# A two-block transformer on one core: adaLN units of four strips in a row, heads of a pair in alternation

## The chip, the core and the metric

The kernel runs on one core of one Trainium2 chip. A core has a matrix engine (PE, whose weight loads are listed apart as PEld), a vector engine (DVE), an activation engine (ACT), a general engine (POOL) and an engine that here only starts transfers (SP); each has its own instruction stream and they meet through semaphores. The metric is the device time of one execution in microseconds (us), the median of several runs of the same program.

## The reference, cut to what matters

Two blocks run one after the other on 256 positions of width 1024. The first has two layers, each with adaLN vectors, a mixer (convolution and a chunked state-space scan, "ssd") and a mixture of experts; its first layer also runs the same on 256 context positions. The second block has four layers, of which the first and the last are forgetting attention ("fox").

```python
def ada_mod(cvec, w_ada, b_ada, n):            # 1024 -> 6 vectors of 1024
    m = jax.nn.silu(cvec) @ w_ada[:, :n * D_MODEL] + b_ada[:n * D_MODEL]
    return jnp.split(m, n, axis=-1)

def first_block(...):
    for l in range(2):
        sh1, sc1, gt1, sh2, sc2, gt2 = ada_mod(c, w_ada[l], b_ada[l], 6)
        # the context: the same with c_ctx
        hx = modulate(rms_norm(h_x, g_mix[l]), sh1, sc1)
        u, gate, z, xbc, dt_raw = split_proj(hx @ p["w_in"])
        xs, bm, cm, dt = ssd_scan_inputs(xbc, dt_raw, p)
        h_x = h_x + gt1 * mixer_output(u, gate, z, xs, bm, cm, dt, a, hf0, hb0, p, rows)
        h_x = h_x + gt2 * hier_moe(modulate(rms_norm(h_x, g_ffn[l]), sh2, sc2), p)
        ...

def ssd_chunked(...):                          # within mixer_output, 8 heads of 64, both directions
    scores = jnp.einsum("bclhn,bcshn->bclsh", cc, bc) * decay_ls
    y_diag = jnp.einsum("bclsh,bcshp->bclhp", scores, xdt)
    ...

def forgetting_attention(h, w_in, b_f, w_out): # 16 heads of 64
    logits = jnp.einsum('bhqd,bhkd->bhqk', q_b, k) * scale
    logits = logits + c_b[..., :, None] - c[..., None, :]
    p = jax.nn.softmax(jnp.where(mask, logits, -jnp.inf), axis=-1)
    return jnp.einsum('bhqk,bhkd->bhqd', p, v) @ w_out
```

## The kernel before

**Arithmetic.** Large products are made of three matmuls of split operands (`mm3`, L45 on): high by high, high by low, low by high. The high part `wh` of a weight is written by ACT from the loaded tile `raw` (L54), the low part `wl` mostly by DVE (L55). All matmuls go through `mm` (L45, L46), so that rows of the profile on them carry L46 and are told apart by the tile they write. A plain fp32 matmul leaves two records on PE, one such as `proj<-xh,wh` one.

**adaLN units.** `ada(l)` (L199) computes silu(c) times `w_ada`: the stationary operand is `sc32`, 128 by 32 (two vectors and 30 zero columns), the moving one a strip of `w_ada`, 128 by 512. A bank of PSUM (`adaps`) takes four strips, one in each quarter of its partitions, that is in each quarter of the array's columns. The generator yields after two strips: this is a *unit* of the kernel before, and two units use one 1 MB load of `w_ada`. `fill(n)` (L264) takes n units and so puts them between other matmuls, wherever it is called: in `load_x`, twice in each projection of the first layer (`proj`, `k in (2, 6)`), in the first layer's ssd, its router and its experts, then in the second layer's z projections, ssd and router. With `hold` (and always at the last of a block) the partial sums leave PSUM for `adar`, by a copy on ACT (L252) or an addition on DVE (L250); `turn` then transposes them into the vectors `AD`.

**ssd.** `head` is a generator of three steps, one for each of 8 heads and stream: step 1 starts the decay logits `L` (a matmul from `pick`), step 2 adds the mask and has ACT write six exponentials into `es` (four slots, L706) which DVE multiplies with `pg`; step 3 multiplies them with `xdt` into `py`. Two heads (a *pair*) share one bank `py`: head e writes partitions 64e to 64e+63, by four matmuls of 64 stationary columns. Three heads are in flight; each step 3 stands by itself in the stream.

**fox.** `heads` handles a pair: for each head in turn `pick`, `cmask` and two `qk` matmuls (64 rows contracted, head e in rows 64e to 64e+63) into a bank of its own; softmax; three transposes per head; and the product with v into one bank, head e in partitions 64e on. Four banks are enough, so the pair's three parts are interleaved with those of the next pair by the caller.

**Order.** A scheduler places instructions in program order with priorities and waits; PE's order, the place of every unit among it, is thus set by where `fill` is called. `moe0` also pins one `fill(1)` behind an instruction (`issue_after(self.placed.ins)`). The experts' weights, the adaLN weights and all others are loaded by one queue of SP in program order into a ring of `raw` buffers.

Of the kernel before, what the change touches and what calls it, by code (L numbers as in the profile page):

```python
# [16 lines left out]
P = 128  # L17
# [12 lines left out]
class Net:  # L30
# [131 lines left out]
    def load_x(self):  # L162
# [8 lines left out]
        self.fill(3)  # L171
# [3 lines left out]
        for k in range(KC):  # L175
            self.ssq_add(k)
            self.fill(1)
# [5 lines left out]
        self.fill(5)  # L183
# [15 lines left out]
    def ada(self, l):  # L199
# [9 lines left out]
        def turn(b, a0, a1):  # L209
# [6 lines left out]
            for a in range(a0, a1):  # L216
                nc.vector.tensor_tensor(o[:, a], pt[:, a, :, 0:2], pv["b_ada"][:, 16 * b + 4 * a:16 * b + 4 * a + 4, None].to_broadcast([P, 4, 2]), op=ALU.add)
            if b != 1 and a0 == 0:
# [4 lines left out]

        blocks = [(b, range(4)) for b in range(3)] if l == 0 else [(0, range(4)), (1, range(4)), (2, range(2)), (2, range(2, 4))]
        for b, groups in blocks:
            groups, n = list(groups), len(groups)
            ps, taken = None, set()

            for k in range(KC):
                for h in range(n // 2):  # L230
                    self.ada_flush()
                    if ps is None:
                        ps, begun = self.pm.tile([P, 512], F32, name="adaps", tag=self.mmtag), set()
                    if h == 0 and (n == 4 or k % 2 == 0):
                        c0 = 2048 * b + 512 * groups[0]
                        r = self.raw(w[:, k:k + 4 // n, c0:c0 + 512 * n], 4 // n, 512 * n)
                    rr = r[:, 0 if n == 4 else k % 2].rearrange("p (g n) -> p g n", n=512)
                    for g in (2 * h, 2 * h + 1):
                        a = groups[g]
                        self.mm(ps[32 * a:32 * a + 32], self.sc32[:, k], rr[:, g], a not in begun, k == KC - 1)  # L240
                        begun.add(a)
                    done = k == KC - 1 and h == n // 2 - 1
                    if done or self.hold:
                        for old in (False, True):
                            part = [a for a in begun if (a in taken) == old]
                            if part:
                                at = slice(32 * min(part), 32 * max(part) + 32)
                                o = rows[at].rearrange("p j n -> p (j n)")
                                if old:
                                    nc.vector.tensor_tensor(o, o, ps[at], op=ALU.add)  # L250
                                else:
                                    nc.scalar.activation(o, ps[at], AF.Copy)  # L252
                        taken |= begun
                        ps = None
                    if done:
                        self.turns.append((turn, b, groups[0], groups[-1] + 1))
                    yield
# [60 lines left out]
    def mixer(self, l):  # L318
# [36 lines left out]
        l0 = [True] + 35 * [False]  # L355
# [33 lines left out]
        for a in range(4):  # L389
            r = self.raw(win[:, :, 1536 + 256 * a:1792 + 256 * a], KC, 256)  # L390
            for b in range(2):
# [5 lines left out]
                if last:  # L397
                    self.fill([0, 0, 0, 0, 0, 0, 0, 0][c])
        for a in range(2):
            r = self.raw(win[:, :, 1024 + 256 * a:1280 + 256 * a], KC, 256)  # L400
            for b in range(2):
# [5 lines left out]
                if last:  # L407
                    self.fill([1, 1, 1, 1][2 * a + b])
# [22 lines left out]
        if last:  # L431
            self.fill(88 - self.units, True)
# [185 lines left out]
    def ssd(self, l, xbc, xdt, cz, dt, dta, rows, NS, ssq, conv, cnorm):  # L618
# [75 lines left out]
        pgs, pys, later = {}, {}, []  # L694

        def head(n, s, c, e):
# [21 lines left out]
            if e == 0:  # L718
                pys[s, c] = pm.tile([P, T], F32, name="py", tag="mm")
            py = pys[s, c]  # L720
            o = py[64 * e:64 * e + 64]
# [1578 lines left out]
```

## Time and profile before

| what | value |
|---|---|
| median of 3 runs | 2184.17 us (2183.2 to 2184.49) |
| the profiled execution | 2185.32 us, its span 2183.5 us |
| PE busy | 2021.5 us, 93% of the span |
| DVE / ACT / POOL busy | 68% / 47% / 20% |
| adaLN matmul records | 384, 89.0 us busy |

The span is the stretch from the first to the last instruction of the profiled execution. PE's busy share is over 99% in long stretches and lower in the first layer's ssd, around the routers and in the second layer's experts. An engine's end of a matmul is modelled, so for what a group of matmuls costs the start of the next instruction on PE is read, not the group's own duration.

### The profile page before, as it was taken

The numbers are of one execution on the slowest core, as the hardware profiler recorded it, in microseconds if no ns is written. First come the engines' busy times: TensorE is split into PE (matmuls) and PEld (weight loads), VectorE is DVE, ScalarE is ACT, GpSimd is POOL, SyncE is SP. The second block draws the span as 40 slices with busy tenths as digits, with TensorE's granted clock in tenths as the row PEclk, the third lists the DMA queues.
The fourth block names the chain that finished last, engine by engine and source line by source line (L and its number), as shares of the span: only waits on it lengthen the run. The fifth ranks groups of instructions, "written<-read, shape, count | busy, mean of one in ns | idle before, by whom it ended". The sixth has DMA issues, their size and how long they took to land.

```text
span 2183.5 us, 37025 instructions
## 1 busy us (share of the span) xinstructions
PE 2021.5 (93%) x14917; PEld 1713.7 (78%) x14919; DVE 1475.4 (68%) x2429; ACT 1034.8 (47%) x1743; POOL 434.4 (20%) x574
## 2 busy tenths in 40 slices
PE   6999896999898989789989997799999999999998
PEld 3655563998586656368889996699998999989998
DVE  4878646999798541069766669976658556667664
ACT  4323543887543631056554452254456444546444
POOL 1000212232433210022268832200001000010000
PEclk9999997999999999999999999799999999999999
DMA  7553414999434479964456653255544554425551
GB/s 297 212 193 117 155 58 150 323 343 338 139 121 149 157 267 366 375 224 155 155 174 203 200 181 103 89 193 174 183 165 136 192 193 157 136 97 195 195 190 39
DMA packets 276595, 408.89 MB, mean 187 GB/s; under 512 B 9856, under 2 KB 241280, under 8 KB 270144
## 3 DMA queue, kind: packets, MB, share of 16 engines
q1 hardware_dynamic: 266976, 380.47, 51.5%
q0 software_dynamic: 8000, 19.67, 2.5%
q10 hardware_dynamic: 1440, 6.29, 0.7%
q8 instruction: 120, 1.97, 0.4%
q14 instruction: 59, 0.48, 0.1%
HBM read 390.93 MB, written 24.64 MB: 190 GB/s over the span
## 4 chain that ended last, share of the span: by engine, by line
PE 48%; DVE 8%; DMA 2%; issue 2%; ACT 2%; POOL 1%; SPq 0%; DVEq 0%; POOLq 0%; ACTq 0%
PE mm L46 43%; DVE wl L55 2%; PE gu L46 2%; PE py L46 1%; DVE Z L2146 1%; DMA raw<-in_w_down 1%; DMA rawe<-in_w_down 1%; PE px L46 1%; DVE gl L1552 1%; DVE A L2139 0%; PE mm L1778 0%; DVE A L2148 0%; PE acc L46 0%; POOL Z L2141 0%; DMA bc<-bcd 0%
## 5 line engine op out<-in xcount | busy, mean ns | idle before, releaser
L54 ACT ACTIVATE wh<-raw 128x1024 fp32r<-128x1024 f32 x490 | 511.1, 1050 | 494.1 <-PE mm L46 274.5
L55 DVE TENSOR_TENSOR wl<-raw,wh 128x1024 fp32r<-128x1024 f32 (+2 forms) x478 | 586.5, 1232 | 223.8 <-ACT wh L54 222.5
L46 PE MATMUL mm<-gh,wh 128*128 128x256 f32 (+1 forms) x1744 | 496.9, 285 | 2.4 <-ACT wh L54 2.4
L46 PE MATMUL mm<-gh,wl 128*128 128x256 f32 (+1 forms) x1744 | 494.0, 283 | 2.3 <-DVE wl L55 2.3
L46 PE MATMUL mm<-gl,wh 128*128 128x256 f32 (+1 forms) x1744 | 493.7, 283 | 0.5 <-DVE gl L1552 0.5
L46 PEld LDWEIGHTS mm<-gh,wh 128*128 128x128 f32 (+1 forms) x1744 | 329.8, 189 | 5.4 <-ACT wh L54 2.6
L46 PEld LDWEIGHTS mm<-gh,wl 128*128 128x128 f32 (+1 forms) x1744 | 329.3, 189 | 3.7 <-DVE wl L55 2.9
L46 PEld LDWEIGHTS mm<-gl,wh 128*128 128x128 f32 (+1 forms) x1744 | 329.6, 189 | 2.2 <-DVE gl L1552 0.9
L46 PE MATMUL mm<-fh,wh 128*128 128x256 f32 x704 | 199.0, 286 | 3.0 <-DVE x L1592 1.6
L46 PE MATMUL mm<-fl,wh 128*128 128x256 f32 x704 | 198.7, 283 | 0.0
L46 PE MATMUL mm<-fh,wl 128*128 128x256 f32 x704 | 198.2, 283 | 0.0
L1556 POOL TENSOR_TENSOR sq<-sq 128x256 f32<-128x256 f32 x48 | 41.2, 859 | 682.7 <-ACT sq L1554 482.5
L46 PEld LDWEIGHTS mm<-fh,wh 128*128 128x128 f32 x704 | 134.2, 192 | 5.1 <-DVE x L1592 2.4
L46 PEld LDWEIGHTS mm<-fl,wh 128*128 128x128 f32 x704 | 134.9, 192 | 0.1
L46 PEld LDWEIGHTS mm<-fh,wl 128*128 128x128 f32 x704 | 134.6, 192 | 0.0
L46 PE MATMUL proj<-xh,wl 128*128 128x512 f32 (+1 forms) x320 | 116.5, 365 | 11.0 <-POOL xr L534 7.7
L46 PE MATMUL proj<-xh,wh 128*128 128x512 f32 (+1 forms) x320 | 120.5, 377 | 1.7 <-ACT wh L54 1.7
L46 PE MATMUL proj<-xl,wh 128*128 128x512 f32 (+1 forms) x320 | 115.4, 361 | 0.0
L46 PE MATMUL gu<-wh,gt 128*128 128x256 f32 x512 | 98.3, 286 | 0.2 <-DVE gt L55 0.2
L46 PE MATMUL adaps<-raw,sc 128*32 128x512 f32 x384 | 89.0, 627 | 9.9 <-DVE sc L170 7.2
L1618 DVE TENSOR_TENSOR ft<-mm,rstd 128x512 f32<-128x512 f32 x88 | 60.8, 691 | 53.3 <-PE mm L46 53.3
L46 PEld LDWEIGHTS proj<-xh,wh 128*128 128x128 f32 x320 | 62.3, 195 | 43.1 <-issue 30.1
(596 smaller groups left out, 4130.7 us busy)
## 6 DMA issues: line engine op xcount, KB each, us to landing
raw<-in_ffn_w_gate_up SPq DMA_DIRECT2D x88, 1024.0 KB, 5.5
raw<-in_w_ada SPq DMA_DIRECT2D x48, 1024.0 KB, 5.0
raw<-in_ffn_w_down SPq DMA_DIRECT2D x44, 1024.0 KB, 4.8
raw<-in_fox_w_in SPq DMA_DIRECT2D x24, 1024.0 KB, 5.9
raw<-in_w_down SPq DMA_DIRECT2D x22, 1024.0 KB, 11.4
raw<-in_w_in SPq DMA_DIRECT2D x20, 1024.0 KB, 5.3
raw<-in_w_gate SPq DMA_DIRECT2D x20, 1024.0 KB, 10.9
raw<-in_w_up SPq DMA_DIRECT2D x20, 1024.0 KB, 12.1
```

Source lines behind the costliest of these rows:

```text
L46: return self.nc.tensor.matmul(out, a, b, start=start, stop=stop, skip_group_check=True)
L54: self.nc.scalar.activation(hi, src, AF.Copy)
L55: (lo_eng or self.nc.vector).tensor_tensor(lo, src, hi.bitcast(F32), op=ALU.subtract)
L1552: nc.vector.scalar_tensor_tensor(self.gl[:, k], x, s, self.gh[:, k].bitcast(F32), op0=ALU.mult, op1=ALU.subtract)
L1556: nc.gpsimd.tensor_tensor(sq, sq, self.sq, op=ALU.add)
L1618: nc.vector.tensor_tensor(t, gu, rs[:, None, :].to_broadcast([P, 2, T]), op=ALU.mult)
L2146: nc.vector.tensor_tensor_scan(z, self.rtab[:, 4 * m:4 * m + 4].rearrange("p a t -> p (a t)"), z, 0.0, ALU.mult, ALU.add)
```

## The change

- `ada`: a unit is now one 1 MB load and its four strips, issued one after the other; there are 48 units in place of 96 half-size ones (24 each layer). The bank leaves PSUM whole.
- Who takes units: `load_x` 2, then one after each second chunk, then 2; each projection of the first layer one (`k == 4`) in place of two; first ssd 2 in place of 4; the first layer's router 1 before and 2 inside in place of 2 and 4; the pinned `fill(1)` of `moe0` is gone; its last call takes 2. In the second layer the z projections take 4 as before, ssd up to 48 in all, and the router none (it took 8 half-size units).
- `head`: the first head of a pair ends after step 2; the second issues both heads' `py` matmuls, alternating between the two halves of the columns.
- `heads` of fox: both heads' `pick` and `cmask` first, then the `qk` matmuls alternating between the two halves of the rows; the product with v alternates too.

```diff
@@ load_x
-        self.fill(3)
+        self.fill(2)
...
-            self.fill(1)
+            if k % 2:
+                self.fill(1)
...
-        self.fill(5)
+        self.fill(2)
@@ ada
-                for h in range(n // 2):
...
-                    for g in (2 * h, 2 * h + 1):
-                        a = groups[g]
-                        self.mm(ps[32 * a:32 * a + 32], self.sc32[:, k], rr[:, g], a not in begun, k == KC - 1)
...
+                r = self.raw(w[:, k, 2048 * b:2048 * b + 2048].rearrange("p (g n) -> p g n", n=512), 4, 512)
+                for a in range(4):
+                    self.mm(ps[32 * a:32 * a + 32], self.sc32[:, k], r[:, a], first, k == KC - 1)
+                if k == KC - 1 or self.hold:
+                    o = rows.rearrange("p j n -> p (j n)")
+                    if taken:
+                        nc.vector.tensor_tensor(o, o, ps, op=ALU.add)
+                    else:
+                        nc.scalar.activation(o, ps, AF.Copy)
+                    ps, taken = None, True
@@ mixer
-                if k in (2, 6) and not last:
+                if k == 4 and not last:
...
-            self.fill(88 - self.units, True)
+            self.fill(48 - self.units, True)
@@ ssd, head
             if e == 0:
-                pys[s, c] = pm.tile([P, T], F32, name="py", tag="mm")
...
-            self.mm(o, xs(0, 0), E[:, 0:2], True, False)
-            self.mm(o, xs(1, 1), E[:, 2:4], False, False)
-            self.mm(o[:, 0:P], xs(0, 1), E[:, 4], False, False)
-            self.mm(o[:, P:T], xs(1, 0), E[:, 5], False, True)
...
+                return
+            py = pm.tile([P, T], F32, name="py", tag="mm")
+            for b, (j, d, cols_) in enumerate(((0, 0, slice(0, 2)), (1, 1, slice(2, 4)), (0, 1, 4), (1, 0, 5))):
+                for q in range(2):
+                    at = slice(b % 2 * P, b % 2 * P + P) if b > 1 else slice(0, T)
+                    self.mm(py[64 * q:64 * q + 64, at], xd(2 * s + j, d)[:, 64 * (2 * c + q):64 * (2 * c + q) + 64],
+                            es[:, (n + q - 1) % 4, cols_], b == 0, b == 3)
@@ ssd, the loop
-            if l == 0 and n in (12, 13, 14, 15):
-                self.fill(1, n == 15)
-            if l == 1 and self.units < 88:
-                self.fill(1, self.units == 87)
+            if l == 0 and n in (12, 14):
+                self.fill(1, n == 14)
+            if l == 1 and self.units < 48:
+                self.fill(1, self.units == 47)
@@ moe0
-            self.fill(2)
-            logits = self.routed(0, NS, f, rows, tmp, pe, lambda k: k % 2, (self.b16("xh"), self.b16("xl")))
+            self.fill(1)
+            logits = self.routed(0, NS, f, rows, tmp, pe, lambda k: k in (2, 6), (self.b16("xh"), self.b16("xl")))
...
-            with tc.issue_after(self.placed.ins):
-                self.fill(1)
...
-                self.fill(4, True)
+                self.fill(2, True)
@@ moe1
-            logits = self.routed(1, 1, f, rows, tmp, pe, lambda k: 1, (xh, xl))
+            logits = self.routed(1, 1, f, rows, tmp, pe, lambda k: 0, (xh, xl))
@@ heads
+        Ls = [self.bank([P, 3, P]) for _ in range(2)]
         for e in range(2):
             h = 2 * c + e
...
+            self.mm(Ls[e], self.pick[:, h:h + 1].to_broadcast([P, P]), c48, True, False)
+            self.mm(Ls[e][:, 0:3:2], self.identb, self.cmask, False, False)
+        for n in range(2):
+            for e in range(2):
+                es = slice(64 * e, 64 * e + 64)
+                if n == 0:
+                    self.mm(Ls[e][:, 0], qk[es, 0, 0:P], qk[es, 1, 0:P], False, False)
+                else:
+                    self.mm(Ls[e][:, 1:3], qk[es, 0, P:T], qk[es, 1], False, True)
```

What stands in a row on PE in a projection of the first layer (tiles: `proj` the projection, `adat` and `adaps` the adaLN vectors and their partial sums; x2 is two matmuls), before:

```order
L46 MATMUL proj<-xl,wh 128x512
L46 MATMUL proj<-xh,wl 128x512
L213 MATMUL adat<-ident,adar 128x128 x4
L46 MATMUL adaps<-raw,sc_127 32x512 x2
L46 MATMUL proj<-xh,wh 128x512
```

and now:

```order
L46 MATMUL proj<-xl,wh 128x512
L46 MATMUL proj<-xh,wl 128x512
L214 MATMUL adat<-ident,adar 128x128 x4
L46 MATMUL adaps<-raw,sc_127 32x512 x4
L46 MATMUL proj<-xh,wh 128x512
```

Four strips stand at one place where two stood, and a projection has one such place where it had two.

PE in the second layer's ssd (`L` decay logits, `py` the heads' product, `ph` and `pg` states and scores), before:

```order
L46 MATMUL pg<-xbc 128x256 x2
L46 MATMUL L<-rt,pick 128x256 x2
L46 LDWEIGHTS identb
L46 MATMUL L<-cm_87,identb 128x512
L46 MATMUL py<-es,xdt 64x256 x2
L46 MATMUL py<-es,xdt 64x128 x2
L46 MATMUL ph<-st 128x256 x4
L46 MATMUL adaps<-raw,sc_127 32x512
L46 MATMUL L<-rt,pick 128x256 x2
```

and now:

```order
L46 MATMUL adaps<-raw,sc_127 32x512 x4
L46 MATMUL L<-rt,pick 128x256 x2
L46 LDWEIGHTS identb
L46 MATMUL L<-cm_87,identb 128x512
L46 MATMUL py<-es,xdt 64x256 x4
L46 MATMUL py<-es,xdt 64x128 x4
L46 MATMUL ph<-st 128x256 x4
L46 MATMUL adaps<-raw,sc_127 32x512 x4
L46 MATMUL pg<-xbc 128x256 x2
```

Eight `py` matmuls of a pair stand together, once in two heads, where four of one head stood at each head.

PE in the last fox layer (`mm` is the bank; `pick`, `cmask` and `qk` are what it is made from, `pt` the transposed softmax), before:

```order
L1778 MATMUL mm<-ident,p 128x128 x6
L46 MATMUL mm<-c_19122,pick 128x384
L46 LDWEIGHTS identb
L46 MATMUL mm<-cmask,identb 128x2x128
L46 MATMUL mm<-qk 128x128
L46 MATMUL mm<-qk 128x256
L46 MATMUL mm<-c_19122,pick 128x384
L46 LDWEIGHTS identb
L46 MATMUL mm<-cmask,identb 128x2x128
L46 MATMUL mm<-qk 128x128
L46 MATMUL mm<-qk 128x256
L46 MATMUL mm<-pt,v 64x256
```

and now:

```order
L1766 MATMUL mm<-ident,p 128x128 x6
L46 MATMUL mm<-c_19115,pick 128x384
L46 LDWEIGHTS identb
L46 MATMUL mm<-cmask,identb 128x2x128
L46 MATMUL mm<-c_19115,pick 128x384
L46 LDWEIGHTS identb
L46 MATMUL mm<-cmask,identb 128x2x128
L46 MATMUL mm<-qk 128x128 x2
L46 MATMUL mm<-qk 128x256 x2
L46 MATMUL mm<-pt,v 64x256 x2
L46 MATMUL mm<-pt,v 64x128 x2
```

The two heads' `qk` matmuls, which `pick` and `cmask` stood between, are neighbours, and so are their products with v of the same width.

## Rows read from the trace of the kernel before

**Rows 1.** Windows: us, busy us (instructions) of PE PEld DVE ACT POOL, clock, DMA share, GB/s.

```profile
60.00:200.00 140.00, 140.00 (x578) 81.90 (x578) 114.88 (x245) 35.46 (x51) 1.18 (x16) 1.00 0.54 185
200.00:290.00 90.00, 79.04 (x352) 47.30 (x352) 54.54 (x105) 55.46 (x142) 24.34 (x29) 0.96 0.32 106
694.00:751.00 57.00, 54.36 (x264) 30.57 (x264) 26.84 (x48) 35.18 (x89) 10.63 (x15) 1.00 0.50 176
795.00:805.40 10.40, 5.79 (x34) 5.48 (x34) 7.87 (x55) 2.78 (x7) 0.00 (x0) 0.51 1.10 349
830.00:930.00 100.00, 87.15 (x614) 48.72 (x612) 12.26 (x44) 13.86 (x25) 7.52 (x8) 0.97 1.07 374
1010.00:1070.00 60.00, 59.79 (x564) 51.49 (x564) 50.74 (x121) 34.88 (x83) 19.24 (x20) 1.00 0.53 177
1890.00:1966.00 76.00, 75.39 (x559) 64.58 (x557) 47.35 (x115) 32.14 (x87) 10.04 (x15) 0.98 0.30 98
```

**Rows 2.** Timeline, first layer's projections: start us, duration, engine, line, tiles, records.

```profile
53.81 1.06 PE L46 MATMUL adaps<-raw,sc 128*32 128x512 f32 x8
54.81 0.51 PE L46 MATMUL proj<-xh,wh 128*128 128x512 f32 x1
...
60.98 0.40 PE L46 MATMUL proj<-xl,wh 128*128 128x512 f32 x1
61.22 0.39 PE L46 MATMUL proj<-xh,wl 128*128 128x512 f32 x1
61.54 1.05 PE L46 MATMUL adaps<-raw,sc 128*32 128x512 f32 x4
62.52 0.50 PE L46 MATMUL proj<-xh,wh 128*128 128x512 f32 x1
62.86 0.39 PE L46 MATMUL proj<-xl,wh 128*128 128x512 f32 x1
```

**Rows 3.** Timeline of a head's product in the first ssd.

```profile
209.66 1.51 PE L46 MATMUL py<-es,xdt 128*64 128x256 f32 x8
...
211.11 0.66 PE L648 MATMUL ptx<-ident,xbc 128*128 128x128 f32 x4
```

**Rows 4.** The exponentials as a tile's row: count, ns min/median/max, first and last start.

```profile
L706 ACT ACTIVATE es<-L,dcol x144: 347/377/494, 205.0 to 733.0; 128x128 f32<-128x128 f32 x144
```

**Rows 5.** Timeline of the first layer's router, DVE; in brackets the wait before.

```profile
374.04 0.69 DVE L250 TENSOR_TENSOR adar<-adar,adaps 128x512 f32<-128x512 f32 x1 [1.69 <-PE adaps L46]
...
375.00 0.15 DVE L1416 TENSOR_TENSOR gidx<-row,far 128x4 int32<-128x4 f32 x1
```

**Rows 6.** Timeline of the end of the second layer's ssd.

```profile
741.32 6.20 PE L46 MATMUL adaps<-raw,sc 128*32 128x512 f32 x26
...
748.47 0.48 ACT L122 ACTIVATE rstd<-ssq,eps 128x256 f32<-128x256 f32 x1
```

**Rows 7.** Timeline of the second layer's router.

```profile
779.59 7.06 PE L46 MATMUL adaps<-raw,sc 128*32 128x512 f32 x32 [0.56 <-ACT rs L290]
...
782.10 0.73 DVE L309 TENSOR_SCALAR mf<-nrm,A,AD 128x256 f32<-128x256 f32 x2
```

**Rows 8.** Chain of waits in the second layer's experts, from 870 us.

```profile
877.50 12.29 DMA raw<-in_w_down
```

**Rows 9.** Transfers issued from 740 to 940 us: count, KB each, us to landing.

```profile
raw<-in_w_ada SPq DMA_DIRECT2D x4, 1024.0 KB, 8.9
```

**Rows 10.** Timeline of the first fox layer.

```profile
1004.82 0.93 PE L46 MATMUL mm<-qk 64*128 64x128 f32 x8
...
1005.68 0.88 PE L46 MATMUL mm<-pt,v 128*64 128x256 f32 x8
...
1006.49 0.33 PE L1994 MATMUL mm<-ident,s5a 128*128 128x128 f32 x1
```

**Rows 11.** Timeline of the last fox layer.

```profile
1913.11 0.92 PE L46 MATMUL mm<-qk 64*128 64x128 f32 x4
...
1913.96 0.44 PE L46 MATMUL mm<-c,pick 128*128 128x384 f32 x1
```

More of the change, by code (lines that the diff above doesn't have):

```diff
@@ L215, in turn @@
             o = AD[:, 16 * b:16 * b + 16].rearrange("p (a j) s -> p a j s", j=4)
-            for a in range(a0, a1):
+            for a in range(4):
                 nc.vector.tensor_tensor(o[:, a], pt[:, a, :, 0:2], pv["b_ada"][:, 16 * b + 4 * a:16 * b + 4 * a + 4, None].to_broadcast([P, 4, 2]), op=ALU.add)
-            if b != 1 and a0 == 0:
+            if b != 1:
                 n, at, gn = (0, 8, "g_mix") if b == 0 else (1, 32, "g_ffn")
@@ L221, in turn @@
                                                op0=ALU.add, op1=ALU.mult)
[L224 to L227, printed above, removed]
+        for b in range(3):
+            ps, taken = None, False
             for k in range(KC):
-                for h in range(n // 2):
[L231 to L237, printed above, removed]
-                    for g in (2 * h, 2 * h + 1):
-                        a = groups[g]
-                        self.mm(ps[32 * a:32 * a + 32], self.sc32[:, k], rr[:, g], a not in begun, k == KC - 1)
[L241 to L257, printed above, removed]
@@ new lines, in ada @@
+                self.ada_flush()
+                first = ps is None
+                if first:
+                    ps = self.pm.tile([P, 512], F32, name="adaps", tag=self.mmtag)
+                r = self.raw(w[:, k, 2048 * b:2048 * b + 2048].rearrange("p (g n) -> p g n", n=512), 4, 512)
+                for a in range(4):
+                    self.mm(ps[32 * a:32 * a + 32], self.sc32[:, k], r[:, a], first, k == KC - 1)
[6 more added lines that the diff above has]
+                    ps, taken = None, True
@@ L1752, in heads @@
         ps = []
+        Ls = [self.bank([P, 3, P]) for _ in range(2)]
         for e in range(2):
             h = 2 * c + e
-            es = slice(64 * e, 64 * e + 64)
-            L = self.bank([P, 3, P])
-            self.mm(L, self.pick[:, h:h + 1].to_broadcast([P, P]), c48, True, False)
-            self.mm(L[:, 0:3:2], self.identb, self.cmask, False, False)
-            self.mm(L[:, 0], qk[es, 0, 0:P], qk[es, 1, 0:P], False, False)
-            self.mm(L[:, 1:3], qk[es, 0, P:T], qk[es, 1], False, True)
+            self.mm(Ls[e], self.pick[:, h:h + 1].to_broadcast([P, P]), c48, True, False)
[7 more added lines that the diff above has]
+                    self.mm(Ls[e][:, 1:3], qk[es, 0, P:T], qk[es, 1], False, True)
+        for e in range(2):
+            L = Ls[e]
             m3, m2 = t("m3", [P, 3]), t("m2", [P, 2])
@@ L1783, in heads @@
         po = self.bank([P, T])
-        for e in range(2):
-            vs = slice(128 * c + 64 * e, 128 * c + 64 * e + 64)
-            o = po[64 * e:64 * e + 64]
-            self.mm(o, v[:, 0, vs], pts[e][:, 0:2].rearrange("p a b -> p (a b)"), True, False)
-            self.mm(o[:, P:T], v[:, 1, vs], pts[e][:, 2], False, True)
+        for n in range(2):
+            for e in range(2):
+                vs = slice(128 * c + 64 * e, 128 * c + 64 * e + 64)
+                o = po[64 * e:64 * e + 64]
+                if n == 0:
+                    self.mm(o, v[:, 0, vs], pts[e][:, 0:2].rearrange("p a b -> p (a b)"), True, False)
+                else:
+                    self.mm(o[:, P:T], v[:, 1, vs], pts[e][:, 2], False, True)
         self.split(oh[:, c], ol[:, c], po)
```

23 lines of the change are left out of this document (10 added, 13 removed).

## The prediction

> **What bounds the kernel now.** I read the page's list of busy times first: PE works 2021.5 of 2183.5 us, so that PE work taken out can shorten the kernel, but not everywhere by the same amount. So the windows by stage come next [rows 1], one for each place that the change touches. The reader is to see three kinds. In the first layer's projections (60 to 200 us) PE is busy all 140.00 us and DVE 114.88: PE bounds, and DVE is the next floor. The last fox layer (1890 to 1966) is the same, 75.39 of 76 with DVE at 47.35. In the two ssd stages PE is busy 79.04 of 90 and 54.36 of 57: some of it is waiting for exponentials and states, so a PE saving is only partly paid out. The first fox layer (1010 to 1070) has PE at 59.79 and DVE at 50.74 of 60, nearly both. The second layer's experts (830 to 930) move 374 GB/s at a DMA share of 1.07: the transfers bound there, and the chain of waits stands 12.29 us on one [rows 8].
>
> Then the timelines, for what one group costs. On PE the start of the next instruction is read.
>
> **The adaLN units.** A run of eight adaLN records (four strips, two records each) starts at 53.81 and the next matmul at 54.81: 1.00 us. A run of four records (two strips) starts at 61.54 and the next at 62.52: 0.98 us [rows 2]. So four strips in a row take what two take; strips in different quarters of the columns run beside each other, but two already fill the slot, the second record of a strip waiting for its first. What a run costs in a projection: 61.22 to 62.86 is 1.64 us for two projection records and the run; two records take 2 x 0.235 (60.98 to 61.22: 0.24) [rows 2]; the run is 1.17.
>
> *First projections.* There are 36 runs between 60 and 200 us before, and the new order has 18, one of them split in two, so 19. 17 x 1.17 = 19.9 us of PE time, all on the bounding engine. But DVE has 114.88 us to do, and 140 - 19.9 = 120.1 leaves it 5 us of slack, so PE will now and then wait for a low part. I take 17. Bounds: 19.9 if DVE never shows, 8 if DVE's work with its waits needs 132.
>
> *The first router.* Before, DVE waits 1.69 us for a unit and adds 0.69 us of `adar` at 374.04, ahead of the index `gidx` at 375.00, from which the gather starts [rows 5]. In the new order the addition comes behind `gidx`, and the pinned unit behind it is gone. I take 2 us, between 0 (the wait falls to something else) and 3.
>
> *The second ssd.* Twelve runs stay twelve, one of them a long block of 26 records at 741.32 [rows 6] that lay beside ACT and DVE work; now they are runs of eight within the loop. Counted alone that is 0, or a loss of up to 2 where the hidden block now lies on the path.
>
> *The second router.* Units stand 7.06 us on PE from 779.59, 32 records, and the router's transposes wait until 786.58 though the first `mf` was ready at 782.10 + 0.37 = 782.47 [rows 7]: 4.1 us. They then wait for the low parts from POOL, some of the 4 us is only moved there. I take 3 (0 to 4). The cover of these units also kept PE at work: the clock granted from 795 to 805.4 is 0.51, that is 1.2 in place of 2.4 GHz, with PE busy 5.79 of the 10.4 us [rows 1]. Without them the lower clock could come sooner; the same work at the full clock would take 2.9 of those 5.79 us, so as long a stretch more of it costs about 3, which is why the lower bound is 0. The Trainium skill, "TensorE: Matmul & The Clock Gate", section "Why this matters for your kernels", advises against idle gaps between bursts of matmuls; by it the sum would lose those 3 us, and no row here shows the router without the units.
>
> **The pairs of heads in ssd.** One head's four `py` matmuls (8 records) take 209.66 to 211.11, 1.45 us [rows 3], and use half of the array's columns. That two heads of a pair, alternating, take the time of one I read from the fox product below. Per pair that is 1.45 saved; where the order leaves the first matmul of the pair alone, its third of the work stays serial: 1.45 - 0.6 = 0.85. The first ssd has 8 pairs, 6 of them so split: 2 x 1.45 + 6 x 0.85 = 8.0 us of PE; one unit run less, 1.0 more. Since PE is busy 79.04 of 90 there, I take 5 of these 9 (0 to 9). The second has 4 pairs, one split: 5.2 us; with PE at 54.36 of 57 I take 4 together with the runs (a loss of 2 to a gain of 7).
>
> **The pairs of heads in fox.** Where two heads' `qk` happen to stand together, eight records take 1004.82 to 1005.68, 0.86 us [rows 10]. In 14 of the 16 pairs of the two fox layers `pick` and `cmask` stand between, and four records alone take 1913.11 to 1913.96, 0.85 [rows 11]. So a head's `qk` beside the other's is free, and 0.85 us a pair is saved. The last layer has 7 such pairs within 1890 to 1966, where PE bounds: 7 x 0.85 = 6.0 (4 to 6.5). The first has 6 within 1010 to 1070: 5.1, of which I take 3.5 (1 to 5), since DVE is nearly as busy.
>
> The product with v gains nothing: eight records take 1005.68 to 1006.49, 0.81 us, in program order head 0, head 0, head 1, head 1 [rows 10]. One head's 256 + 128 columns alone would take half of a `py` head's 768, 1.45 / 2 = 0.73, so the two already run beside each other almost whole.
>
> **The sum.** 17 + 5 + 2 + 4 + 3 + 3.5 + 6 = 40.5 us. The profiled execution took 2185.3 (span 2183.5 and 1.8 around it), giving 2144.8; the median is 1.15 lower, so 2143.7, and I forecast 2143.5. With all terms at their better ends (19.9 + 9 + 3 + 7 + 4 + 5 + 6.5 = 54.4) it is 2130, at their worse (8 + 0 + 0 - 2 + 0 + 1 + 4 = 11) 2173.
>
> **Rivals.**
> - *DVE's floor in the first projections.* DVE is already at 82% there [rows 1], and it must finish a weight's low part before PE can go on; if its chain with ACT takes 132 us, only 8 of the 17 are paid: 2152.5. For it: few slack microseconds (5 of 120). Against: DVE's queue has no wait of its own there that PE's order makes longer.
> - *Stages with latency pay nothing.* Both ssd, both routers and the first fox layer wait for ACT, DVE or a transfer all the same; only 17 + 6 remain: 2161. For it: PE's idle share there; against: 54.36 of 57 is not much idle.
> - *The experts' transfers end earlier.* Four 1 MB loads of `w_ada` are issued after 740 us [rows 9], in the queue ahead of the experts' weights. In the new order they stand earlier. If the experts are bound by the queue from its start, 4.2 MB at 374 GB/s [rows 1] come off: 11.2 us in place of the 3 of the router, 2135. Against: most of the weights start only when the buffers come free after the router.
> - *The pair waits on its exponentials* (slower). The even head's `es` slot is now kept one step longer, until the pair's `py`; of four slots two then wait. If ACT had to stop for them, six exponentials of 0.377 us [rows 4], 2.26, and the pair's `py` of 1.45 would come in series in each pair: 3.7 us x 12 pairs = 44.5, which gives 2188. It decides above 40.5 / 12 = 3.4 us per pair. Against: the slot of head n is asked for at step n + 4, and is free after step n + 3.
> - *Matmuls start in program order.* If head 1's first product with v could start only after head 0's second has, 256 + 256 + 128 columns would lie in series before and 256 + 128 now; of 0.81 us that is 0.32 a pair, 16 x 0.32 = 5 us in the two fox layers: 2138.5. Against: the 0.81 us are one head's time already. The Trainium skill, "TensorE: Matmul & The Clock Gate", section "Part 3: Packing small matmuls — row/col tiling", has this rule: matmuls keep strict order, and only weight loads are pulled ahead. By it the sum would be 5 higher; the row of 0.81 us disagrees.
> - *Nothing but moves*: PE finds other waits in all stages, 2184.
>
> **How the numbers follow.** Forecast 0.42; DVE's floor 0.21; latency stages 0.14; transfers 0.14; program order 0.02; the exponentials 0.04; no change 0.03. The range takes in the forecast, DVE's floor, the transfers and the nearer half of the latency case: 2130 (the better ends of all terms) to 2162, leaving out 0.07 + 0.04 + 0.03 and some of the tail below, under 0.2. A measurement of this kernel can tell 0.2% (4.4 us) from no change: faster than that are all cases but the last two, 0.93; the same 0.03; slower 0.04.
>
> **What would show it.** Right: the stretch from the first projection to the first ssd 15 to 20 us shorter, with DVE near 95% busy there; `py` groups of 16 records in about 1.5 us; `qk` groups of 8 in 0.86 at every fox pair; transposes of the second router some 4 us after its reciprocal. Wrong: if PE in the first projections shows idle time for `wl` (DVE's floor), if `es` shows waits for PE (exponentials), if a stage after an unchanged length begins only with a transfer's landing, or if eight records of one unit take 2 us where its weights change with each strip.

## The result

The changed kernel takes 2134.32 us (median, 2133.03 to 2138.56) where the kernel before took 2184.33: a ratio of 0.9774, 95% interval 0.9757 to 0.9791, 50.0 us less. The forecast was 2143.5 with a range of 2130 to 2162; direction and range hold, the gain was 50 where 40.5 were summed.

The page of the changed kernel, its first lines (span, busy time by engine, which answer to the table on the profile before):

```profile
span 2131.5 us, 37017 instructions
PE 1963.7 (92%) x14915; PEld 1696.5 (80%) x14915; DVE 1472.7 (69%) x2429; ACT 1036.9 (49%) x1742; POOL 437.1 (21%) x574
```

PE gave up 57.8 us of busy time, and the span 52.0. DVE's and ACT's busy times are unchanged within 3 us: nothing was computed less, PE alone was relieved.

Where the 52.0 us of the span went is read by taking the same DVE instruction in both traces and subtracting its starts. Columns: the stretch in the time of the kernel before, the change of its length in the changed kernel, and the same for three kernels that carry one part of the change each (next section); negative is shorter.

| stretch | changed | adaLN alone | ssd alone | fox alone |
|---|---|---|---|---|
| first projections, 53 to 204 | -19.85 | -19.85 | 0.00 | 0.00 |
| first ssd, 204 to 293 | -8.34 | -0.69 | -8.85 | +1.64 |
| first output projection, 293 to 346 | -1.54 | -1.53 | -1.53 | -1.51 |
| first router, 346 to 410 | -1.15 | -1.42 | -0.37 | +0.90 |
| second ssd and its output, 683 to 780 | +1.22 | +3.32 | -0.10 | +0.03 |
| second router, 780 to 804 | +0.39 | +0.38 | +0.01 | +0.01 |
| second experts, 804 to 951 | -4.99 | -4.51 | -0.01 | +0.15 |
| first fox layer, 951 to 1102 | -3.89 | -0.28 | -0.05 | -4.29 |
| start of its feed-forward, 1102 to 1142 | -4.44 | -1.84 | +0.07 | -1.66 |
| last fox layer, 1885 to 1974 | -9.24 | -1.59 | -1.60 | -9.14 |

What is left out of it sums to -0.2 in the changed kernel. Where kernels that have no edit near a stretch show the same -1.5 or -1.6, it is the profiled execution of before that was longer there, not they that were shortened by an edit: its granted clock is 0.66 from 296 to 301 us and 0.72 from 1893 to 1899. A difference of that size can go the other way too. The kernel with fox alone has no edit ahead of the fox layers and is 1.64 longer in the first ssd, where its granted clock is 0.66 from 210 to 215 us and before's is 1.00, and 0.90 longer in the first router. So a row under some 1.6 us shows no gain by itself.

**First projections.** The windows are those of before, of the changed kernel, and of a kernel that moves all units out of the stretch (a6 below); columns as in [rows 1].

```profile
53.26:203.60 150.34, 150.34 (x626) 88.53 (x627) 122.67 (x263) 43.78 (x61) 1.18 (x16) 1.00 0.54 184
```

```profile
53.90:184.37 130.47, 130.47 (x625) 87.61 (x626) 122.49 (x263) 43.75 (x61) 1.18 (x16) 1.00 0.62 216
```

```profile
93.20:224.10 130.90, 116.76 (x508) 90.66 (x506) 122.62 (x261) 50.74 (x76) 1.16 (x16) 0.97 0.20 66
```

The reader is to see PE busy all the time in the first two, and DVE's busy time the same in all three. 150.34 - 130.47 = 19.87: 17 runs by 1.17.

**The pairs.** Timeline of the first ssd in the changed kernel, which answers to [rows 3]: both heads, 16 records, take 1.45 us as one head's eight did.

```profile
223.91 1.52 PE L46 MATMUL py<-es,xdt 128*64 128x256 f32 x16
225.36 0.73 PE L46 MATMUL pA<-erow,pick 128*128 128x256 f32 x4
```

Timeline of a pair in the last fox layer, which answers to [rows 11]:

```profile
1865.90 0.42 PE L46 MATMUL mm<-c,pick 128*128 128x384 f32 x1
1866.16 0.28 PE L46 MATMUL mm<-cmask,identb 128*128 128x256 bf16 x1
1866.20 0.42 PE L46 MATMUL mm<-c,pick 128*128 128x384 f32 x1
1866.46 0.28 PE L46 MATMUL mm<-cmask,identb 128*128 128x256 bf16 x1
1866.67 0.93 PE L46 MATMUL mm<-qk 64*128 64x128 f32 x8
1867.53 0.65 PE L46 MATMUL mm<-pt,v 128*64 128x256 f32 x4
```

Eight `qk` records take 1866.67 to 1867.53, 0.86 us, where two heads took 0.85 each. Besides, the second `pick` follows the first `cmask` after 0.04 us, and only the change from `cmask` (all rows) to `qk` (64 rows) takes 0.21; before, there were two such changes a pair. So a pair takes 3.01 us from its transposes to the end of the product with v where it took 4.05: 1.04 less in each of six of the seven pairs of the last layer that `pick` and `cmask` had parted; the first of the seven, whose `qk` also waits for DVE (0.61 us before, 0.31 now), is 1.34 shorter. In the first layer they had parted five pairs, not six as the prediction counted: 12 of the 16, not 14.

### The profile page after: what moved, and what is told of

Read it like the earlier page. It is cut to its first block, busy times and chain, and to the rows that moved or that the text cites. A ratio compares the mean times of both kernels' runs of the same rounds, so it can differ in the third digit from the quotient of the medians.

```text
span 2131.5 us, 37017 instructions
## 1 busy us (share of the span) xinstructions
PE 1963.7 (92%) x14915; PEld 1696.5 (80%) x14915; DVE 1472.7 (69%) x2429; ACT 1036.9 (49%) x1742; POOL 437.1 (21%) x574
## 4 chain that ended last, share of the span: by engine, by line
PE 48%; DVE 9%; DMA 2%; issue 2%; ACT 1%; POOL 1%; SPq 0%; DVEq 0%; POOLq 0%; ACTq 0%
PE mm L46 43%; DVE wl L55 2%; PE gu L46 2%; PE py L46 1%; DVE Z L2137 1%; DMA rawe<-in_w_down 1%; PE px L46 1%; DVE gl L1533 1%; DMA raw<-in_w_down 1%; DVE A L2130 0%; PE mm L1766 0%; DVE A L2139 0%; DVE s5a L2088 0%; POOL Z L2132 0%; DMA bc<-bcd 0%
## 5 line engine op out<-in xcount | busy, mean ns | idle before, releaser
L54 ACT ACTIVATE fh<-fa 128x256 fp32r<-128x256 f32 x88 | 36.7, 417 | 111.6 <-DVE fa L1602 111.6
## 6 DMA issues: line engine op xcount, KB each, us to landing
raw<-in_w_down SPq DMA_DIRECT2D x22, 1024.0 KB, 11.2
raw<-in_w_up SPq DMA_DIRECT2D x20, 1024.0 KB, 11.2
```

The costliest lines, as they stand in the source:

```text
L54: self.nc.scalar.activation(hi, src, AF.Copy)
```

## The experiments

All are compared with the kernel before on the same chip; ratios carry their 95% interval.

**The parts alone.** Three kernels take one part of the change each.

d1, the adaLN part (`ada` and every place of `fill`), `head` and `heads` as before:

```diff
 kernel before, with
+ ada(), fill() in load_x, proj, ssd, moe0, moe1 as in the change
  head(), heads() unchanged
```

> The kernel before with the adaLN part alone: units of four strips, the new places of units, none in the second layer's router; the products of ssd and fox stay head after head. Theory (a matmul run taken out of a stretch that PE bounds pays its own 1.17 us): 19.9 us in the first layer's projections, 1 in the first ssd, 1 in the first router, about 4 in the second layer's experts, 0 in the second ssd: 25 to 27 us faster than before, 2157 to 2159. Rival (the whole gain of 50 is from ssd and fox, and DVE's floor eats the units): 8 to 12 us, 2172 to 2176.

2158.37 us, ratio 0.9889 (0.9872 to 0.9905): 24.9 faster, a hair below the theory's 25 to 27. The rival is out. One term of the theory is out too: the second ssd, put at 0, is 3.32 longer.

d2, the pairing of `py`:

```diff
 kernel before, with
+ head(): the pair's eight py matmuls at its second head, alternating
```

> The kernel before with the pairing of the py products in ssd alone. Theory: the first ssd is bound by PE and pays all 8.0 us of its pairs, the second ssd is set at its end by ACT and POOL and pays 0 to 2: 8 to 10 us faster, 2174 to 2176. Rival (the stages wait for exponentials all the same): 0 to 4 us faster, 2180 to 2184.

2173.07 us, ratio 0.9959 (0.9945 to 0.9973): 10.2 faster. In the table it stands where the theory put it, -8.85 in the first ssd, -0.10 in the second; the other 1.5 is the stretch in which before's profiled execution was longer.

d3, the pairing in fox:

```diff
 kernel before, with
+ heads(): both heads' pick and cmask first; qk and the product with v alternating
```

> The kernel before with the pairing in fox alone. Theory: each pair that pick and cmask separated saves 1.04 us (0.85 of qk and 0.19 of one change between the whole array and its halves), 7 x 1.04 in the last layer and some 5 x 1.04 in the first, with up to 4 more from the clock after the first fox layer: 12 to 17 us faster, 2167 to 2172. Rival (only the qk matmuls' own time, 0.85 a pair, and half of it lost in the first layer): 8.5 to 9.5 us, 2175.

2171.83 us, ratio 0.9945 (0.9928 to 0.9961): 11.4 faster, just below the 12 to 17 of the theory and above the rival's 9.5. The traces carry the mechanism (1.04 a pair, see above) and show what is missing: in the first layer five pairs bring 5 x 1.04 = 5.2 and 4.29 are left at its end.

The three sum to 24.9 + 10.2 + 11.4 = 46.5 of the 50.0; the rest is within what the intervals (about 3.5 us each) allow. Two rows do not add up: the second ssd (3.32 and -0.10 against 1.22) and the start of the feed-forward (-1.84, 0.07 and -1.66 against -4.44); both are taken up in the next section.

**Alternation or neighbourhood?** a1 keeps fox's new grouping but lets the heads follow in turn:

```diff
-        for n in range(2):
-            for e in range(2):
+        for e in range(2):
+            for n in range(2):
```

> The changed kernel with pick and cmask of both heads first as there, but qk and the product with v head after head (head 0's two, then head 1's two) in place of alternating. Theory (halves run beside each other wherever they are neighbours, the order within is free): the same time as the changed kernel within 1 us, eight qk records in 0.86 us and eight of v in 0.81. Rival (matmuls start strictly in program order, so only alternating neighbours overlap): head 1's first waits for head 0's second, about 0.3 us a pair for qk and as much for v, 16 x 0.6 = 10 us slower than the changed kernel, 2144.

2136.3 us, ratio 0.9767 (0.9749 to 0.9786) beside 0.9774 of the changed kernel: the same. Timeline of a pair of it:

```profile
1873.13 0.93 PE L46 MATMUL mm<-qk 64*128 64x128 f32 x8
1873.99 0.88 PE L46 MATMUL mm<-pt,v 128*64 128x256 f32 x8
1874.80 0.39 PE L46 MATMUL mm<-gh,wh 128*128 128x256 f32 x1
```

0.86 us for `qk` and 0.81 for the product with v, as when they alternate (0.86 and 0.80). In fox the alternation is worth nothing; that the two heads are neighbours is all of it.

a2 does the same to the eight `py` matmuls of an ssd pair, four of one head, then four of the other:

```diff
-            for b, (j, d, cols_) in enumerate(...):
-                for q in range(2):
+            for q in range(2):
+                for b, (j, d, cols_) in enumerate(...):
```

> The changed kernel with the ssd pair's eight py matmuls head after head in place of alternating (the scheduler may part them more). Theory (neighbours overlap whatever the order): where all 16 records stand together they take 1.45 us as in the changed kernel, and pairs that the order parts lose up to 1.45 each. Rival (strict program order): 16 records together take (256 + 256 + 128 + 128) + (256 + 128 + 128) columns or more, 2.4 us and up.

2143.53 us, ratio 0.9814 (0.9791 to 0.9838). Here the theory falls: where all 16 records stand together,

```profile
225.26 2.43 PE L46 MATMUL py<-es,xdt 128*64 128x256 f32 x16
227.62 0.62 PE L46 MATMUL pA<-erow,pick 128*128 128x256 f32 x3
```

they take 2.36 us against 1.45 alternating, near the rival's 2.4, and so in all five such groups of this run. But the rival's reason is not quite it either. In the single records of this group the first head's eight start at 225.26, 225.53, 225.74, 225.96, 226.17, 226.28, 226.39 and 226.50, and the second head's first starts at 226.18: behind five of them and ahead of three that precede it in the program. The second head runs ahead, but by three records only: the second record of the first head's third matmul and both of its fourth. That settles both runs: a fox head has four records for `qk` and four for the product with v, and three are passed, so that order costs nothing there; a `py` head has eight, and order decides. The whole is 9 us slower than the changed kernel, of which its first ssd takes 4.2 and its second 3.3. The Trainium skill, "TensorE: Matmul & The Clock Gate", section "Part 3: Packing small matmuls — row/col tiling", says that matmuls keep strict program order and only weight loads are pulled ahead; by that the second head would have started no earlier than the first head's fourth matmul, at 226.39, and the group would, by an estimate from these starts, have taken 1.13 + 1.45 = 2.58 us or more. The trace differs: 2.36, and three records were passed.

**Is there more to take in ssd?** In the changed kernel six of the first ssd's eight pairs still issue one matmul alone, since the first head's data are ready a step earlier. a4 lets the second head go first in each alternation, so that none can go ahead:

```diff
-                for q in range(2):
+                for q in (1, 0):
```

> The changed kernel, but in ssd the pair's second head goes first in each alternation, so that no first matmul of a pair can be issued ahead of the rest and stand alone. Theory (a lone first matmul costs the pair 0.58 us, and the first ssd is bound by PE): six pairs of the first ssd, 6 x 0.58 = 3.5 us, faster than the changed kernel by 2 to 4 us, 2130 to 2132. Rival (the lone matmuls stand in PE time that waits for exponentials anyway): within 1 us of the changed kernel, 2133 to 2135.

2140.23 us, ratio 0.9801 (0.9784 to 0.9817): slower than the changed kernel by about 6, 3.7 of them in the first ssd. Its trace is 3.2 us ahead of the changed kernel's by 243 us (0.5 of it from ahead of the stage) and 3.2 behind it at the reciprocal of the stage's end (262.39 there, 265.58 here). Windows of its tail, and of the changed kernel's:

```profile
240.00:255.00 15.00, 10.53 (x46) 6.36 (x47) 6.04 (x11) 8.44 (x17) 2.73 (x4) 0.66 0.01 4
```

```profile
240.00:252.50 12.50, 9.15 (x52) 5.28 (x51) 8.95 (x14) 11.87 (x26) 5.09 (x6) 1.00 0.25 84
```

The granted clock is 0.66 where it was 1.00. Two runs ask what that did. a7 reverses the order in the context's four pairs alone, so that the tail stays as it was:

```diff
-                for q in range(2):
+                for q in ((1, 0) if s else (0, 1)):
```

> The changed kernel with the pair's second head first in the four pairs of the context stream alone; the other four pairs of the first ssd, whose order the run with all pairs changed lost its gain, stay as in the changed kernel. Theory (a lone first matmul costs 0.58 us of PE time, and the earlier loss came from the tail's clock): 2 to 3 us faster than the changed kernel, 2131 to 2132, if the tail keeps the granted clock at 1.00. Rival (the pairs' order shifts who waits for the exponentials and the gain is lost again in the tail): same or up to 3 us slower.

2134.43 us, ratio 0.9772 (0.9746 to 0.9798): the same as the changed kernel, as the rival had it; but the trace shows the theory's gain, made and lost again. The context's four pairs now stand whole, and from 225 to 243.5 us every DVE instruction comes 2.19 us earlier than in the changed kernel (0.45 of it from ahead of the stage). Then the theory's condition fails: the tail, whose order is the changed kernel's, is granted 0.73 from 240.00 to 252.50 us, not 1.00. Timeline of a piece of it in the changed kernel:

```profile
246.12 1.08 PE L46 MATMUL py<-es,xdt 128*64 128x256 f32 x10
247.13 1.13 PE L46 MATMUL pz<-xbc,st 128*128 128x256 f32 x4
```

and in a7:

```profile
244.92 1.97 PE L46 MATMUL py<-es,xdt 128*64 128x256 f32 x10
246.82 2.08 PE L46 MATMUL pz<-xbc,st 128*128 128x256 f32 x4
```

The ten records take 1.90 us where they took 1.01, and at 252.6 us the lead is gone. In both kernels PE waits 2.83 us for `es` just before; the clock falls after it in a7 alone.

a8 keeps all pairs reversed and puts three runs of idle matmuls, read by nobody, into the tail:

```diff
+            if l == 0 and n in (14, 16):
+                self.idle()          # four 128x32 by 512 matmuls
+                if n == 14:
+                    self.idle()
```

> The kernel with the second head first in all pairs, and three runs of four 128x32 by 512 matmuls that nobody reads in the tail of the first ssd, two ahead of the 3.0 us that PE waits there and one ahead of the 1.5 us. Theory (the 7.9 us lost in that tail are the lower clock, 0.66 granted from 240 to 255 us, which follows PE's waits): the clock stays above 0.9 there and 4 to 6 us come back, 2134 to 2136. Rival (the tail is a chain of DVE, ACT and POOL whatever the clock): 2140 or more, with the runs in the way.

2142.27 us, ratio 0.9807 (0.978 to 0.9834). Its window:

```profile
240.00:255.00 15.00, 10.63 (x55) 5.50 (x52) 7.20 (x12) 10.31 (x20) 4.19 (x5) 0.77 0.13 46
```

The clock rose only to 0.77 and the stage is as long as a4's (4.57 against 4.62 us shorter than before's). So the experiment did not do what it set out to do. Of the 6.3 us that a4 loses in its tail, a7 puts some 2 on the clock, without any change of order there; whether the rest is a4's longer stretch at the low clock or the order of its last pairs stays open.

**The second router.** The units that stood there before can't go back, since a unit of four strips now holds the scale that the router needs. a3 puts eight idle runs in their place, one after each chunk:

```diff
             self.mm(pl, wrs[:, k], xl[:, k, :NT], False, k == KC - 1)
+            if l:
+                self.idle()
             self.fill(nf(k))
```

> The changed kernel with eight runs of four 128x32 by 512 matmuls in the second layer's router, one after each chunk, whose results nobody reads: the cover that the units gave PE there before. Theory (router bound by DVE, POOL and ACT; the cover lies beside them and keeps the clock at its higher level): same or up to 2 us faster than the changed kernel, 2132 to 2134, granted clock in the router above 0.9 where the changed kernel has 0.66. Rival (what stands on PE there is in the transposes' way): 3 to 5 us slower, 2137 to 2139.

2140.93 us, ratio 0.9804 (0.9784 to 0.9824). Windows of the router, of it and of the changed kernel:

```profile
750.30:768.90 18.60, 18.21 (x98) 5.49 (x99) 11.82 (x26) 6.55 (x18) 6.96 (x10) 1.00 1.01 352
```

```profile
750.50:765.60 15.10, 7.65 (x33) 5.51 (x34) 11.86 (x25) 6.39 (x18) 7.05 (x10) 0.66 1.00 348
```

The cover keeps the clock at 1.00, and the router takes 3 us longer all the same: PE, 18.21 of 18.60 busy, has become its bound. The clock of 0.66 costs the changed kernel less than these runs do. As a test of the units that stood there before it is weak: those were one block ahead of the transposes, these are scattered among them, and some take 2.1 us.

**How far do units matter in the first projections?** a6 runs all 18 of that stretch right after `load_x`:

```diff
-        self.fill(2)
+        self.fill(19)
+        self.fill(1, True)
...
-                if k == 4 and not last:
-                    self.fill(1, l0.pop())
```

> The changed kernel with the 18 units of the first layer's projections run ahead of them, right after the units of load_x. Only the length of the projections' stretch is read (55 to 184 us in the changed kernel, some 129 us). Theory (PE still sets the pace with 18 runs left): taking them out shortens the stretch by 18 x 1.17 = 21 less what DVE's floor takes back; DVE was at 94% busy, so 7 to 10 us come off and DVE is then 98% busy or more. Rival (PE bound all the way): 19 to 21 us come off.

The whole takes 2173.08 us, as the 18 loads now stand ahead of everything. The stretch itself (its window is above) takes 130.90 against 130.47: nothing came off. Theory (7 to 10) and rival (19 to 21) are both out. PE is now idle for 14 us of it, most of that waiting for `wl` (6.8 us) and `wh` (4.1), and DVE is busy for the same 122.62 us. PE's projections run up to 13 us ahead of the changed kernel's, two thirds into the stretch, and give most of that back in these waits. So the stretch needs some 130.5 us whatever PE does, for DVE's work and its waits, and the changed kernel stands just there: PE's load was brought down to that floor and no further. That it is DVE's floor is read from its busy share and from who waits for whom; no run lightens DVE.

**Units elsewhere.** a9 moves four of the second layer's units from its ssd into its projections, a10 eight (and takes over a7's order):

```diff
                 step(5)
+                if last and c % 2:       # a10: if last
+                    self.fill(1)
```

> The changed kernel with four units of the second layer moved from its ssd into its projections (behind every second of the eight xbc pieces), where PE was busy 32.2 of 40 us. Theory (in ssd units cost their PE time, 3.3 us by the run with the adaLN part alone; in the projections DVE and POOL set the pace and units are free): 2 to 4 us faster than the changed kernel, 2130 to 2132. Rival (the second ssd's end is set by ACT and POOL, or the units' loads come in the way of the weights' in the projections): 0 or slower, 2134 to 2137.

2145.76 us (2140.32 to 2153.45), ratio 0.9828 (0.979 to 0.9866): slower.

> The changed kernel with eight units of the second layer in its projections and the second head first in the context's pairs. Theory: the gains of the two edits add up, 4 to 6 us faster than the changed kernel, 2128 to 2130. Rival: 2134 or more, as in the single runs' rivals.

2138.51 us, ratio 0.98 (0.977 to 0.9829): slower or the same. In both the second layer's ssd and output come later than in the changed kernel, by some 10 and 2 us at the reciprocal of the second router, with PE waiting 10.1 and 10.0 us there for ACT's squares (2.8 in the changed kernel). So taking units out of the second ssd did not shorten it; why it grew longer is not settled. PE's time there is not free all the same: in a2 three groups in it take 0.91 us more each, and the stage is 3.3 longer.

No kernel tried is faster than the changed one beyond its interval.

## Why the prediction was right, step by step

*The units in the first projections: the mechanism right, the term 3 us short.* 17 runs by 1.17 were summed to 19.9, and 17 taken for fear of DVE. 19.85 came. The discount was wrong, and so was the rival: its floor of 132 us was for the 140 us of [rows 1], of which by the same 19.85 some 120 are left. The floor of the whole stretch is 130.5 (a6), and the sum just reaches it. The runs are 36 in the stretch from 53 to 204 us; from 60 to 200, as the prediction has it, there are 34.

*The first ssd: the largest of the mis-sized terms.* 5 of 9 us were taken, since PE was busy 79.04 of 90 there. 8.85 came from the pairing alone (d2), for which 8.0 had been summed; 8.34 in the changed kernel. The list of waits of PE in the kernel before, 200 to 290 us (total us, times, longest), has its two largest as

```profile
PE py L46 <- DVE es L715: 3.4, 3, 2.2
PE L L46 <- ACT es L706: 2.8, 3, 1.8
```

three waits each. The 11 us of idle time are a few longer waits; between them PE was busy without a gap, and there a removed microsecond was paid in full. a7 agrees: its context's pairs, no longer parted, pay there too.

*The second ssd: gained in part, and lost right behind.* A gain of 4 was taken; the row grew 1.22. Up to the first matmul of the output projection (`wout`) the changed kernel is 1.44 shorter, though its granted clock there is 0.72 from 658 to 664 us; a3 and a7, whose program up to there is the same in this stage, keep 1.00 and have -0.02 and 0.18 in the row. The output projection then loses 2.66: it takes 28.50 us from its first matmul's start to its last's where it took 25.84. The first matmul before and in the changed kernel:

```profile
751.11 0.37 PE L46 MATMUL wout<-mh,wh 128*128 128x256 f32 x1
```

```profile
719.34 0.58 PE L46 MATMUL wout<-mh,wh 128*128 128x256 f32 x1 [4.79 <-ACT mh L54]
```

Windows from there on, before and in the changed kernel:

```profile
751.00:758.00 7.00, 7.00 (x60) 6.97 (x59) 5.68 (x13) 3.08 (x6) 1.32 (x2) 1.00 0.65 254
```

```profile
719.40:724.50 5.10, 4.87 (x20) 4.42 (x21) 4.91 (x8) 2.08 (x7) 2.93 (x4) 0.50 0.00 0
```

Before, the long block of units [rows 6] kept PE at work beside ACT's last waits, and the projection starts at the full clock, its matmuls 0.12 us apart. Now PE has nothing to do for 4.79 us, the granted clock is 0.50, and up to 724.5 us its matmuls are mostly 0.21 apart. The parts show whose doing it is: d2 and d3 leave the units where they were and take 25.79 and 25.84 us for the projection; d1 moves them, waits the same 4.79, and takes 28.69. That is 2.85 of its 3.32. So the step that failed here is that the block counted as hidden work that could be moved for 0 to 2; the cover that it gave to PE, which the prediction weighed for the router's units alone, was left out of this term. Ahead of the projection d1 is 0.47 longer and the changed kernel 1.44 shorter: beside units in the loop the pairing gains 1.9 there, by itself (d2) nothing.

*The second router: a term that wasn't there.* 3 us were taken from the 4.1 that the transposes waited behind the units [rows 7]. The router is 0.39 longer. In the changed kernel the first transposes come early,

```profile
753.53 1.09 PE L1281 MATMUL xt<-ident,mf 128*128 128x128 f32 x4 [3.62 <-DVE mf L295]
```

but the last `mf` starts at 763.04, 12.6 us after the reciprocal at 750.45; before it started at 791.80, 12.2 after 779.57. So the chain of DVE, ACT and POOL over the chunks sets it, with or without the units; the price of 3 for the lower clock did not come either. Of the two bounds (0 and 4) the lower held.

*The experts' transfers: the rival that came to pass, in part.* Four loads fewer after 740 us were priced at 11.2 with the weights' queue as the bound, or 0. It was 4.99, and 4.51 with the adaLN part alone. The timeline of before shows a wait at the start of the stage,

```profile
809.68 4.41 PE L46 MATMUL gu<-raw,gt 128*64 128x256 f32 x32
815.98 1.94 PE L46 MATMUL gu<-raw,gt 128*64 128x256 f32 x14 [1.88 <-issue]
```

that is gone after,

```profile
780.54 1.92 PE L46 MATMUL gu<-raw,gt 128*64 128x256 f32 x14
782.61 4.09 PE L46 MATMUL gu<-raw,gt 128*64 128x256 f32 x32
786.63 0.39 PE L46 MATMUL px<-ohr,th 128*128 128x256 f32 x1
```

which is 2.3 us, and the rest of the 5 us comes off along the stream. In the sum it takes the place of the router's 3. That this rival's time, 2135, is the nearest to the measured one is chance: less than half of its 11.2 came.

*Fox: right, with a piece not seen.* 0.85 a pair was predicted, 1.04 measured; the other 0.19 is the change from all rows to half of them that a pair now makes once, not twice. In the last layer that is 6 x 1.04 and once 1.34, 7.6 of the 9.24; the other 1.6 is a lower clock in before's profiled execution (its step between matmuls is 0.21 us at 1895.74, where it is 0.12 at the higher level), which d1 and d2 lack too. In the first layer 3.5 was taken of 5.1 for six pairs; they are five, with 5.2 by the measured price, and 3.89 came. The product with v gained 0.01 a pair, as the prediction had it.

*The first router* was put at 2 and gave 1.15. The index `gidx` comes 2.2 us earlier against the start of the stage, as was read from [rows 5], but at the stage's end no more is left than kernels without an edit there differ by (d2 -0.37, d3 +0.90): the term is not shown.

*What wasn't in the sum at all: the clock.* At about 1116 us the kernel before falls to the lower level for some 10 us, after its feed-forward has waited 2.39 and 1.42 us for its first weights:

```profile
1115.00:1120.00 5.00, 3.58 (x18) 3.39 (x17) 5.00 (x6) 4.18 (x5) 3.33 (x5) 0.60 0.50 161
1120.00:1125.00 5.00, 3.70 (x17) 3.41 (x17) 3.59 (x5) 1.67 (x3) 4.61 (x9) 0.50 0.18 61
```

The changed kernel, which waits 1.04 and 1.42 us there, does the same work at the full clock:

```profile
1077.00:1082.00 5.00, 2.95 (x23) 2.75 (x23) 5.00 (x7) 4.64 (x7) 4.26 (x6) 1.00 0.62 208
```

That is 3.0 of the 4.44 us in that row of the table, which come off between 1118 and 1130 us of before; the other 1.4 are gone ahead of it, with the shorter first wait. d2, which leaves everything near it as it was, has the lower clock like before; in d1, d3 and a1 the 5 us from about 1117 are granted 0.66 and the next 1.00, and a3 keeps 1.00 throughout; there the same piece gains 2.1 (d1), 2.0 (d3) and 3.1 (a3). With the 1.5 us of the first output projection and the 1.6 of the last fox layer some 6 of the 52 us are clock that before's profiled execution was not granted, and not work that was removed. Some 4 went the other way, 1.4 in the second ssd and 2.7 in its output projection.

Put together: 19.85 for 17, 8.3 for 5, 1.15 for 2, -1.2 for 4, -0.4 for 3, 5.0 for 0, 3.9 for 3.5, 9.2 for 6, and 4.4 + 1.5, most of it clock, for 0. The large terms and their mechanisms held; that the total lies so well inside the range is in part luck, since two terms of 7 together brought a loss of 1.6, and 11 us came that the sum did not have.

## What to carry to other kernels

Work that uses a half or a quarter of the array's rows or columns should stand beside its complement; whether it must alternate depends on how many records one side has in a row: with four here the order cost nothing, since three were passed; with eight it cost 0.91 us a pair. What a removed run pays is read from what the stage's next engine needs with its waits, not from that engine's busy share: PE's load can be cut down to that floor in full, and beyond it for nothing. A filler that stands beside a wait of other engines is free, and it may pay besides: the block that was taken from ahead of the second output projection left PE idle for 4.79 us there, and the lower clock behind that cost 2.7. It does not always pay: in the second router the filler of a3 kept the clock up and cost 3.

## What the runs showed of the hardware that was not expected

- Matmuls of the other half of the columns started ahead of three records that precede them in the program (226.18 against 226.28, 226.39 and 226.50), not ahead of more; so in all five groups of a2.
- A change from a matmul on all rows to one on 64 rows took 0.21 us from start to start, where two matmuls on all rows into different banks followed each other after 0.04.
- The tail of the first ssd, the same instructions on PE in the same order behind the same wait of 2.83 us, ran at a granted clock of 1.00 in the changed kernel and of 0.73 in a7, which differs from it only in pairs 30 us and more ahead; the lower clock cost 2.2 us.
- The same feed-forward start ran over 5 us at a granted clock of 0.50 in d2, 0.66 in d1 and 1.00 in a3, at a price of up to 3 us.
